# Exchanging two projections between attention stages: group B's queries go to stage B, group C's gate goes to stage A

## The chip, the core and the metric

The kernel runs on one core of one Trainium2 chip. The metric is the device time of one execution in microseconds: the median of three runs of the kernel before is 923.14 us (922.13 to 925.34). Engines have short names: PE is TensorE's matmuls and PEld its weight loads, DVE is VectorE, ACT is ScalarE, POOL is GpSimd, SP is SyncE, which here issues the DMAs.

## What is computed

Two layers of one block, on 512 latent tokens and 256 context tokens of width 1024, one batch, float32:

```
h  = rms_norm(x, norm_g[l]) * (1 + sc) + sh          # hc likewise from ctx
qa, ka, va, ga, qb, kb, vb, gb, qn, kn, vn, gn = split(h @ w_in[l])
ya = rms_norm(diff_attend(rope(norm(qa)), ka_all, va_all, lam)) * (1 - lam_init) * silu(ga)
yb = gqa_attend(rope(norm(qb)), kb_all, vb_all) * silu(gb)
yn = neighbourhood_attend(norm(qn), norm(kn), vn, kn_c, vn_c, rpb) * silu(gn)
x  = x + gt * (concatenate([ya, yb, yn]) @ w_out[l])
```

Group A is differential attention with 4 heads of 64 (two score maps each), group B is grouped-query attention with 6 query heads on 2 key heads, group C is neighbourhood attention with 6 heads, a window of 8 x 16 and a learned bias. Latent queries also attend to all context keys. In layer 0 the context stream has attention and an update of its own; in layer 1 it has only keys and values left to give.

## The kernel before, in words

**Tiles.** Tokens are cut into six tiles of 128, numbered j: 0 to 3 are latent, 4 and 5 are context. The columns of the input projection are cut into chunks (`CH`): `b0` is keys and values of group B, `b1` its queries, `gb` its gate, `c0`, `c1`, `c2` are keys, values and queries of group C, `gn` its gate. `b1`, `gn`, `gb`, `c0`, `c1` and `c2` are 384 columns wide. In layer 1 `b1`, `c2` and the gates have latent tiles only (`ctx_cols`, line 647).

**One projection tile** (`proj`, line 709): 24 matmuls, three for each of eight slices of the inner dimension (lines 679 to 681), because inputs and weights are split into a high and a low part. It is yielded in four quanta. Then `evac` (line 657) takes the result from its PSUM bank, of which the pool psP has two, which it shares with a few small uses. Weights come as pieces (`WStream`, line 60): SP loads raw, ACT makes the high part (line 89), POOL or DVE the low part (line 92). Six pieces are held; a piece is split when an old one is done with. In stage A all low parts fall to POOL, in stage B every second one goes to DVE (`VSHARE`).

**Evacuation of queries or keys** (`qk_evac`, line 451): ACT copies the tile into one of five buffers named xn (462) and squares it (464), DVE sums the squares (465). For group A and B's latent tiles POOL does the turn of the rotary embedding: two products into tb, one of two buffers (485, 487), a product (489, every fourth one on DVE) and a sum (490); other keys, and B's context queries, get one product on POOL (492). After every second tile, or the last, POOL raises the pair's means to the power -1/2 (163); then for each tile DVE scales (498), ACT casts to float16 (515, 523), DVE takes the rest (516, 524), and SP issues a transposing DMA into stB or a big tile (530, 531, 534), from which the scores read.

**Evacuation of a gate** (`gate_evac`, line 597): tanh on ACT (600), one operation on DVE into tb (602), and a DMA into the DRAM tensor g_d (606). `gate_load` (964) brings it back when a unit group needs it; if it isn't there yet, `attn` pumps the projections on.

**Attention units** (`attn`, line 975): scores on PE into one of two psS tiles (775), maximum on DVE (830; 827 with the bias for group C), exponent on ACT (844), high part on ACT (864), low part on POOL (865), a transposing DMA into pt (867), values on PE (900, 901), evacuation (906). The low part is one step behind the scores and the values four steps. Group A also combines its two maps on DVE (860).

**Stages and order.** `both` (line 1054) runs the units of one group and, in between, a list of chunks (`fill`, line 1031), so that after each unit a due share of the quanta has been emitted. Stage A runs group A's units with the list `FA`, stage B group B's with `FB`, stage C group C's with `FC` (turning of outputs and the output projection). `both` has a parameter `lead`, which is 0 everywhere: so many quanta are emitted ahead of the first unit. The order of the weight pieces follows the same lists (`ORDER`). When the list of stage B is through, the high and low inputs are free and the outputs' tiles take their place (line 1073). Group C's bias table is loaded into the buffer that held group B's queries and keys (lines 984 to 987). The emitted program is then ordered for each engine at compile time by a list scheduler with a timeline of its own (line 1353); scores have a priority 400 places ahead of their place (line 779). Each engine then runs its own list in that order.

```
FA = ["b0", "b1", "gb"]
FB = ["c0", "c1", "c2", "gn"]
...
js = (4, 5, 0, 1, 2, 3) if c == "gn" else range(6)
...
both(l, "A", FA)
both(l, "B", FB)
```

Of the kernel before, what the change touches and what calls it, by code (L numbers as in the profile page):

```python
# [116 lines left out]
def tile_hybrid_block(ctx: ExitStack, tc: tile.TileContext, xT_d, cT_d, ng_d, w_ada, bT_d, w_in, w_out,  # L117
# [11 lines left out]
    def sb(shape, dt=F32, tag="", bufs=1):  # L129
        return pool.tile(shape, dt, tag=tag, bufs=bufs, name=tag)  # L130
# [38 lines left out]
    def big(s, dt=F32, shape=None):  # L169
        return sb(shape or [128, KT, SW[s]], dt, "bigL" if s == 0 else "bigC", 3)  # L170
# [89 lines left out]
        next(st["ada"], None)  # L260


    FA = ["b0", "b1", "gb"]
    FB = ["c0", "c1", "c2", "gn"]
    FC = ["y", "o"]
    YE = 2
    F1 = ["a1", "ga"]
    ORDER = [c for c in ["a0"] + F1 + FA + FB + FC if c in CH]
    VCOL = {"a0": (256, 384), "a1": (0, 128), "b0": (128, 256), "c1": (0, 384)}
# [13 lines left out]
    for l in range(DEPTH):  # L283
        for c in ORDER:
            n, c0 = CH[c][1], sum(v[1] for k, v in CH.items() if k < c)
# [96 lines left out]
    def open_norm():  # L382
        nbuf["t"] = sb([128, 2 * NT], F32, "stB")
# [225 lines left out]
    def open_y(l):  # L609
        for k in "hl":  # L610
            yT[k] = [big(0, F32R)] + ([big(1, F32R)] if l == 0 else [])
# [35 lines left out]
    def ctx_cols(l, c):  # L647
        n = CH[c][1]
        if l == 0:
            return n  # L650
        return {"a0": 384, "a1": 128, "b0": 256, "b1": 0, "c0": 384, "c1": 384, "c2": 0}.get(c, 0)

    def tiles_of(l, c):
        js = (4, 5, 0, 1, 2, 3) if c == "gn" else range(6)
        return [(j, CH[c][1] if j < 4 else ctx_cols(l, c)) for j in js if j < 4 or ctx_cols(l, c)]

    def evac(l, c, j, n, ps, last, tag=None):
# [74 lines left out]
    def units(l, g):  # L732
        us, cs = [], []
        for j in range(4):
            for u in range(4 if g == "A" else NH[g]):
                us.append(dict(g=g, j=j, lat=True, segs=[2 * u, 2 * u + 1] if g == "A" else [u]))
        if l == 0:
            for j in (4, 5):
                if g == "A":
                    cs += [dict(g=g, j=j, lat=False, segs=[2 * h, 2 * h + 1]) for h in range(4)]  # L740
                else:
                    cs += [dict(g=g, j=j, lat=False, segs=[3 * i, 3 * i + 2, 3 * i + 1]) for i in range(2)]
        return cs + us if g == "C" else us + cs
# [279 lines left out]
    def run(gen):  # L1023
        for _ in gen:
            pass

    def n_quanta(l, chunks):
        return sum(4 * len(tiles_of(l, c)) if c in CH else (6 if l == 0 else 4) * 2 if c == "y" else
                   8 if c == "n" else 8 * (4 if l == 0 else 2) for c in chunks)

    def fill(l, toks):
        for c in toks:
            if c in CH:
                yield from proj(l, [c])
            elif c == "y":
                n = 6 if l == 0 else 4
                for j in range(0, n, 2):
                    y_pair(l, j)
                    yield
                    yield  # L1040
                for j in range(n):
                    if (l, "B", j) not in turned:
                        y_build(l, "gb", j)
                    yield
            elif c == "n":
                for db in range(KT):
                    while any((l, "C", j) not in turned for j in range(3)):
                        yield
                    out_head(l, db)
                    yield  # L1050
            else:
                yield from out_parts(l)

    def both(l, g, chunks, lead=0):
        share.phase = g
        f = fill(l, chunks)
        nf = n_quanta(l, chunks)
        na = len(units(l, g)) + 4
        for _ in range(lead):
            next(f, None)  # L1060
        done = [lead]

        def pump():
            next(f)
            done[0] += 1

        st["pump"] = pump
        for x, _ in enumerate(attn(l, g)):
            want = min(nf, lead + (nf - lead - REST.get(g, 0)) * (x + 1) // (na - (YE if g == "B" else 0)))
            while done[0] < want:  # L1070
                next(f, None)
                done[0] += 1
            if g == "B" and done[0] >= nf and st.get("y") != l:
                run(f)
                open_y(l)
                st["y"] = l
        run(f)
# [115 lines left out]
    if True:  # L1193
        cT = sb([128, KT, 2], F32, "cT")
        SP.dma_start(out=cT, in_=cT_d)
        x = [big(0), big(1)]
        for h in range(4):
            for st_, t0, w in streams:
                SP.dma_start(out=x[st_][:, 2 * h:2 * h + 2, :], in_=xT_d[:, 2 * h:2 * h + 2, t0:t0 + w])

        warm = psS.tile([128, 1024], F32, tag="s", name="warm")
        for h, n in ((1, 2), (2, 1), (3, 1)):
            for _ in range(n):
                PE.matmul(warm[:, 0:512], lhsT=ident, rhs=x[0][:, 2 * h, :], start=True, stop=True)
        SP.dma_start(out=ng, in_=ng_d)
        SP.dma_start(out=bT, in_=bT_d)
        V.tensor_tensor(out=sel, in0=ident[:, 0:2], in1=ident[:, 32:34], op=ALU.add)
        V.tensor_tensor(out=sel, in0=sel, in1=ident[:, 64:66], op=ALU.add)
        V.tensor_tensor(out=sel, in0=sel, in1=ident[:, 96:98], op=ALU.add)
        th = sb([128, KT, 2], F32, "th")  # L1210
        A.activation(out=th, in_=cT, func=AF.Tanh, scale=0.5)
        V.tensor_scalar(out=th, in0=th, scalar1=1.0, scalar2=0.5, op0=ALU.add, op1=ALU.mult)
        V.tensor_tensor(out=cS[:, :, 0:2], in0=th, in1=cT, op=ALU.mult)
        V.tensor_scalar(out=bT1, in0=bT[:, :, 8:16], scalar1=1.0, scalar2=None, op0=ALU.add)
        open_norm()
        for kt in range(KT):
            for st_ in range(2):
                norm_acc(x[st_][:, kt, :], kt, st_, True)
        ada0 = [ada_load(0, (8, 0))]
        W.advance(1)  # L1220
        for kt in range(1, KT):
            ada0.append(ada_load(0, (8 + kt, kt), kt % 3 == 2))
            if kt % 2 == 1 and kt < 7:
                W.advance(kt // 2 + 2)
        ada_pair(ada0[0])
        rs = norm_both()
        for st_ in range(2):
            hT[st_] = (big(st_, F32R), big(st_, F32R))

        def before0(gi, kt):  # L1230
            if kt:
                ada_pair(ada0[kt])
            for st_ in range(2):
                build_h(0, st_, kt, x[st_], rs[st_])
            if kt == 5:
                layer_consts(0)

        st["ada"] = ada_blocks([(0, b) for b in range(16, 24)] + [(1, b) for kt in range(KT) for b in (8 + kt, kt)]
                               + [(1, b) for b in range(16, 24)])
        share.phase = "1"  # L1240
        proj_first(0, "a0", [[0, 1, 2, 3, 4, 5]], before0)
        for _ in range(AK[0][0] + 1):
            ada_step()
        for l in range(DEPTH):
            share.phase = "1"
            st["cad"] = AK[l][1]
            run(fill(l, F1))
            st["cad"] = AK[l][2]
            both(l, "A", FA)
            st["cad"] = AK[l][3]  # L1250
            both(l, "B", FB)
            while st["done"] < (24 if l == 0 else 32):
                ada_step()
            st["cad"] = 0
            both(l, "C", FC + ["n"] * (l + 1 == DEPTH))
            if l + 1 == DEPTH:
                out_tail(l)
                break
            x = [big(0), big(1)]
            open_norm()  # L1260
            rs = [None, None]
            for db in range(KT):
                out_final(l, db, 1, x[1])
            rs[1] = norm_finish(1)
            for db in range(KT):
                out_final(l, db, 0, x[0])
            hT[1] = (big(1, F32R), big(1, F32R))
            for kt in range(KT):
                prio(-800)(build_h)(l + 1, 1, kt, x[1], rs[1])

            def before1(gi, kt):
                if gi == 1:
                    if kt == 0:
                        rs[0] = norm_finish(0)
                        hT[0] = (big(0, F32R), big(0, F32R))
                    prio(-800)(build_h)(1, 0, kt, x[0], rs[0])

            proj_first(1, "a0", [[4, 5], [0, 1, 2, 3]], before1)
# [81 lines left out]
```

## Time and profile before

| what | us |
|---|---|
| median of three runs | 923.14 |
| the profiled execution's own time | 924.36 |
| its span, first to last instruction | 922.5 |
| mean granted TensorE clock | 0.952 of full speed |
| layer 0: first scores of group A, of B, latent ones of C | 108.5, 260.3, 408.0 |
| layer 1: the same | 599.5, 722.8, 807.9 |

A row of the profile gives line, engine, operation and tiles (written <- read, by the program's names), shapes, how often, then busy time and mean, then the idle time of the engine just before with what ended it. A row in order of time gives start and duration in microseconds first. In a row of a stretch of time each engine's busy microseconds stand with its number of instructions in brackets, then the granted clock, the DMA engines' mean busy share, and GB/s. A letter q behind an engine's name is its sequencer.

### The profile page before, as it was taken

What the parts mean: (1) busy time and instruction counts of PE and PEld (TensorE: products, weight loads), DVE (VectorE), ACT (ScalarE), POOL (GpSimd) and SP (SyncE); (2) the same over time, 40 slices, a digit from 0 to 9 for tenths busy, and PEclk for the clock granted to TensorE, in tenths of its full rate; (3) what the DMA queues carried; (4) which work ended last, traced back from release to release, by engine and by line L of the source; (5) the groups of instructions that cost most, each with busy time, mean ns of one, the idle gap of its engine ahead of it and who ended that gap; (6) DMA issues with size and microseconds to landing.
All of it is one profiled execution on the core that took longest, in us unless ns stands there. A gap on an engine that the chain in (4) does not pass through costs nothing. (4 is left out here: it accounts for less than half of the span.)

```text
span 922.5 us, 17964 instructions
## 1 busy us (share of the span) xinstructions
PE 825.3 (89%) x6386; PEld 706.9 (77%) x6386; DVE 679.0 (74%) x1306; ACT 592.4 (64%) x1269; POOL 541.3 (59%) x502
## 2 busy tenths in 40 slices
PE   5898997996998899897999989989959999988988
PEld 3787876895987789785778889879849878865767
DVE  5985787988678866558656797789877967656843
ACT  5334577784887687477653445478758988839830
POOL 2638855899698565435330047938988886634420
PEclk9899999998999999898999989989969999997989
DMA  9834895645979996998898713784557899996642
GB/s 328 306 97 126 202 214 141 139 95 134 193 162 222 202 223 173 219 259 215 184 211 237 258 52 101 185 185 102 133 128 175 149 190 246 231 260 171 152 91 83
DMA packets 307049, 165.46 MB, mean 179 GB/s; under 512 B 256528, under 2 KB 275216, under 8 KB 306704
## 3 DMA queue, kind: packets, MB, share of 16 engines
q1 hardware_dynamic: 306960, 164.33, 73.7%
q8 instruction: 50, 0.82, 0.4%
q14 instruction: 39, 0.32, 0.1%
HBM read 86.55 MB, written 15.47 MB: 111 GB/s over the span
## 5 line engine op out<-in xcount | busy, mean ns | idle before, releaser
L865 POOL TENSOR_TENSOR hl<-p,hl 128x768 f16<-128x768 f32 (+3 forms) x138 | 203.6, 1480 | 164.9 <-ACT hl L864 148.8
L679 PE MATMUL proj<-whi,bigL 128*128 128x384 f32 (+1 forms) x592 | 203.0, 344 | 8.4 <-DVE tb L602 4.2
L680 PE MATMUL proj<-wlo,bigL 128*128 128x384 f32 (+1 forms) x592 | 199.4, 337 | 0.8 <-POOL wlo L92 0.7
L681 PE MATMUL proj<-whi,bigL 128*128 128x384 f32 (+1 forms) x592 | 197.3, 335 | 0.0
L844 ACT ACTIVATE p<-sc,nb,gsc 128x768 f32<-128x768 f32 (+3 forms) x200 | 166.4, 846 | 10.6 <-DVE p L860 4.7
L830 DVE TENSOR_REDUCE mx<-sc 128x1 f32<-128x768 f32 (+2 forms) x128 | 118.7, 932 | 33.2 <-PE sc L775 33.0
L679 PEld LDWEIGHTS proj<-whi,bigL 128*128 128x128 f32 x592 | 115.2, 195 | 18.7 <-DVE tb L602 5.9
L864 ACT CAST hl<-p 128x768 f16<-128x768 f32 (+3 forms) x144 | 104.1, 726 | 38.5 <-DMA pt<-hl 22.5
L680 PEld LDWEIGHTS proj<-wlo,bigL 128*128 128x128 f32 x592 | 115.5, 195 | 3.9 <-POOL wlo L92 1.5
L681 PEld LDWEIGHTS proj<-whi,bigL 128*128 128x128 f32 x592 | 114.6, 194 | 2.8 <-issue 2.0
L92 POOL TENSOR_TENSOR wlo<-raw,whi 128x768 fp32r<-128x768 f32 (+1 forms) x44 | 83.4, 1902 | 40.3 <-ACT whi L89 37.5
L89 ACT CAST whi<-raw 128x768 fp32r<-128x768 f32 (+1 forms) x104 | 80.3, 780 | 28.4 <-DMA raw<-in_w_in_dram 14.0
L900 PEld LDWEIGHTS <-pt 128*128 128x128 f16 x736 | 65.5, 99 | 35.3 <-DMA pt<-hl 20.9
L679 PE MATMUL proj<-whi,bigC 128*128 128x384 f32 (+2 forms) x224 | 76.0, 339 | 1.0 <-ACT xn L462 1.0
L92 DVE TENSOR_TENSOR wlo<-raw,whi 128x768 fp32r<-128x768 f32 (+1 forms) x60 | 64.9, 1085 | 15.9 <-ACT whi L89 14.4
L680 PE MATMUL proj<-wlo,bigC 128*128 128x384 f32 (+2 forms) x224 | 74.8, 334 | 0.0
L163 POOL TENSOR_TENSOR rsqb<-rsqb,half 128x12 f32<-128x12 f32 (+2 forms) x25 | 68.4, 2737 | 10.0 <-DVE rsqb L162 9.2
L681 PE MATMUL proj<-whi,bigC 128*128 128x384 f32 (+2 forms) x224 | 74.1, 333 | 0.0
L901 PEld LDWEIGHTS <-pt 128*128 128x128 f16 x736 | 66.0, 100 | 4.3 <-issue 2.2
L832 ACT ACTIVATE nb<-mx,lnp,gsc 128x1 f32<-128x1 f32 (+1 forms) x104 | 39.7, 386 | 36.5 <-DVE mx L830 24.4
L775 PE MATMUL sc<-bigL 128*128 128x512 f16 (+4 forms) x184 | 46.4, 312 | 18.0 <-ACT p L844 17.2
L900 PE MATMUL pv<-vA,pt 128*128 128x128 f16 (+2 forms) x424 | 51.3, 228 | 9.6 <-DMA pt<-hl 9.2
(320 smaller groups left out, 2031.5 us busy)
## 6 DMA issues: line engine op xcount, KB each, us to landing
raw<-in_w_in_dram SPq DMA_DIRECT2D x64, 384.0 KB, 4.0
adw<-in_w_ada_dram SPq DMA_DIRECT2D x68, 256.0 KB, 3.6
raw<-in_w_out_dram SPq DMA_DIRECT2D x16, 384.0 KB, 4.7
raw<-in_w_in_dram SPq DMA_DIRECT2D x16, 256.0 KB, 3.1
g_d<-tb SPq DMA_DIRECT2D x20, 192.0 KB, 2.7
gt<-g_d SPq DMA_DIRECT2D x18, 192.0 KB, 3.4
hl<-in_w_ada_dram SPq DMA_DIRECT2D x12, 256.0 KB, 5.2
pt<-in_w_ada_dram SPq DMA_DIRECT2D x12, 256.0 KB, 5.2
```

The source lines that it names most:

```text
L89: self.nc.scalar.copy(out=hi, in_=raw2)
L92: self.share("W").tensor_tensor(out=lo, in0=raw2, in1=hi.bitcast(F32), op=ALU.subtract)
L163: G.tensor_tensor(out=y, in0=x, in1=half[:, 0:n], op=ALU.pow)
L679: PE.matmul(ps, lhsT=xh, rhs=hi, start=(kt == 0), stop=False)
L680: PE.matmul(ps, lhsT=xh, rhs=lo, start=False, stop=False)
L681: PE.matmul(ps, lhsT=xl, rhs=hi, start=False, stop=(kt == KT - 1))
L830: V.tensor_reduce(out=mx[:, 0:ns], in_=ps[:, 0:w * ns].rearrange("p (a b) -> p a b", b=w), axis=AX.X, op=ALU.max)
L844: A.activation(out=p[:, w * x:w * x + w], in_=u["ps", i][:, w * x:w * x + w], func=AF.Exp, bias=u["nb", i][:, x:x + 1], scale=lc[l]["sc"][ ...
L864: A.copy(out=hl[:, 0:n], in_=p)
L865: lo_eng.tensor_tensor(out=hl[:, n:2 * n], in0=p, in1=hl[:, 0:n], op=ALU.subtract)
L900: PE.matmul(po[r, :], lhsT=pt[:, b, r], rhs=V_[:, vt, c0:129], start=first, stop=False)
L901: PE.matmul(po[r, 0:65 - c0], lhsT=pt[:, nb + b, r], rhs=V_[:, vt, c0:65], start=False, stop=stop)
```

## The change

`b1` leaves `FA` and becomes the first chunk of `FB`; `gn` leaves the end of `FB` and takes the place of `b1` in `FA`. Stage B is given a lead of nine quanta, which is two tiles of `b1` and the first quarter of the third. `c2`, now the last chunk of `FB`, gets the tile order that `gn` had, context tiles first; `gn` keeps it. Nothing else is touched: the same tiles are projected and evacuated by the same instructions.

```diff
-    FA = ["b0", "b1", "gb"]
-    FB = ["c0", "c1", "c2", "gn"]
+    FA = ["b0", "gn", "gb"]
+    FB = ["b1", "c0", "c1", "c2"]
...
-        js = (4, 5, 0, 1, 2, 3) if c == "gn" else range(6)
+        js = (4, 5, 0, 1, 2, 3) if c in ("c2", "gn") else range(6)
...
             both(l, "A", FA)
             st["cad"] = AK[l][3]
-            both(l, "B", FB)
+            both(l, "B", FB, 9)
```

## The prediction

> **What bounds the kernel now.** I read the page first, for the busy shares, then cut the trace into the attention stages, then into ten-microsecond pieces, and last read single engines in order of time where the pieces stood out.
>
> ```profile
> PE 825.3 (89%) x6386; PEld 706.9 (77%) x6386; DVE 679.0 (74%) x1306; ACT 592.4 (64%) x1269; POOL 541.3 (59%) x502
> ```
>
> TensorE leads, so time is lost only where it stops or slows. The stages follow from where the scores run; the scores of stage B are the ones that read stB:
>
> ```profile
> L775 PE MATMUL sc<-stB x216: 269/273/390, 260.3 to 804.4; 128*128 128x512 f16 x96, 128*128 128x256 f16 x12
> ```
>
> The next rows give length, then busy time with instructions of PE, PEld, DVE, ACT, POOL, then the granted clock. They are, in layer 0, stage A, two pieces of it and stage B; then the same four of layer 1.
>
> ```profile
> 108.00:260.00 152.00, 133.07 (x1032) 116.87 (x1032) 128.29 (x213) 115.37 (x297) 116.31 (x117) 0.97 0.71 161
> 208.00:218.00 10.00, 5.71 (x38) 4.65 (x39) 10.00 (x9) 3.21 (x8) 10.00 (x6) 1.00 0.44 94
> 218.00:228.00 10.00, 7.31 (x29) 6.34 (x28) 7.14 (x10) 6.61 (x16) 9.16 (x7) 0.66 0.72 214
> 260.00:408.00 148.00, 137.11 (x1151) 119.01 (x1150) 101.97 (x192) 106.47 (x187) 89.41 (x64) 0.98 0.91 207
> 600.00:723.00 123.00, 106.46 (x748) 94.97 (x747) 102.88 (x157) 94.89 (x220) 96.74 (x96) 0.90 0.60 140
> 670.00:680.00 10.00, 2.16 (x15) 1.11 (x14) 6.75 (x7) 7.34 (x18) 10.00 (x7) 0.65 0.43 100
> 680.00:690.00 10.00, 7.18 (x27) 6.49 (x25) 8.76 (x11) 3.55 (x10) 8.05 (x8) 0.50 0.45 121
> 723.00:808.00 85.00, 81.75 (x666) 70.60 (x665) 62.45 (x94) 72.94 (x122) 63.76 (x43) 1.00 1.02 214
> ```
>
> Each stage A has one twenty-microsecond hole in TensorE while POOL is full. Elsewhere stage A of layer 0 does (1032-67) matmuls in 132 us, 7.31 a microsecond; the 67 in the hole are worth 9.2 us, so the hole costs 10.8. In layer 1 it is (748-42)/103 = 6.85 a microsecond, 42 are worth 6.1, and the hole costs 13.9. Together 24.7 us. Stage B has no such hole: TensorE is busy 137 of 148 and 82 of 85 us.
>
> What fills POOL in the first hole, and what VectorE does then:
>
> ```profile
> 208.80 1.99 POOL L92 TENSOR_TENSOR wlo<-raw,whi 128x768 fp32r<-128x768 f32 x1
> 210.75 1.33 POOL L489 TENSOR_TENSOR xn<-xn,t1Bq 128x384 f32<-128x384 f32 x1
> 212.04 3.95 POOL L92 TENSOR_TENSOR wlo<-raw,whi 128x768 fp32r<-128x768 f32 x2
> ```
> ```profile
> 212.09 2.19 DVE L516 TENSOR_TENSOR stg<-xn,stg 128x384 f16<-128x384 f32 x1
> 214.20 2.59 DVE L860 SCALAR_TENSOR_TENSOR p<-p,dn,p 128x768 f32<-128x768 f32 x1
> ```
> ```profile
> 219.26 0.59 PE L775 MATMUL sc<-bigL 128*128 128x512 f16 x1 [3.33 <-ACT p L844]
> ```
> ```profile
> 683.87 0.69 PE L679 MATMUL proj<-whi,bigL 128*128 128x384 f32 x1 [2.81 <-DVE tb L602]
> ```
>
> POOL is turning group B's queries (t1Bq) between weight splits (L92). VectorE's two-input operations stretch beside it, maxima and exponents come late, and TensorE waits for a score bank (3.33 us) or, in layer 1, for a gate tile's tb, a buffer that the turn of the queries uses too (2.81 us). How far the stretch belongs to a busy POOL is shown by the subtraction of line 516 in stage A of layer 0, where it follows group B's queries, and then in stage B:
>
> ```profile
> L516 DVE TENSOR_TENSOR stg<-xn,stg 128x384 f16<-128x384 f32 x6 | 7.6, 1267 | 1.3 <-ACT stg L515 1.2
> ```
> ```profile
> L516 DVE TENSOR_TENSOR stg<-xn,stg 128x384 f16<-128x384 f32 x6 | 3.1, 550 | 1.5 <-ACT stg L515 1.5
> ```
>
> 1267 ns against 550 for the same work.
>
> **The change, part by part.** TensorE's projections cancel: gn and b1 are both 384 columns wide, six tiles each in layer 0 and four in layer 1. So do the weights: as many pieces are loaded and split in each stage, in the same place of the stream. What changes places is the evacuation. For group B's queries POOL has
>
> ```profile
> L485 POOL TENSOR_TENSOR tb<-xn,t2Bq x8: 582/623/922, 184.6 to 676.8; 128x192 f32<-128x192 f32 x8
> L487 POOL TENSOR_TENSOR tb<-xn,t2Bq x8: 590/602/1296, 185.2 to 677.3; 128x192 f32<-128x192 f32 x8
> ```
> ```profile
> L489 POOL TENSOR_TENSOR xn<-xn,t1Bq x6: 996/1004/1330, 192.8 to 683.4; 128x384 f32<-128x384 f32 x6
> ```
> ```profile
> L163 POOL TENSOR_TENSOR rsqb<-rsqb,half 128x12 f32<-128x12 f32 x4 | 9.4, 2359 | 0.4 <-DVE dn L858 0.4
> L492 POOL TENSOR_TENSOR xn<-xn,gs 128x384 f32<-128x384 f32 x4 | 4.2, 1046 | 0.1
> L490 POOL TENSOR_TENSOR xn<-xn,tb 128x384 f32<-128x384 f32 x4 | 4.0, 1008 | 0.0
> ```
>
> The four latent tiles of a layer cost 4 x (0.62 + 0.60 + 1.01) + 3 x 1.00 (one product in four of line 489 is VectorE's) = 11.9 us. Layer 0 adds two context tiles, 2 x 1.05, and three powers, 3 x 2.36: 21.1 us in all. Layer 1 has two powers: 16.6 us. A gate tile has nothing on POOL, one tanh on ScalarE and on VectorE
>
> ```profile
> L602 DVE SCALAR_TENSOR_TENSOR tb<-sq,proj 128x384 f32<-128x384 f32 x4 | 2.2, 555 | 7.7 <-ACT sq L600 7.7
> ```
>
> 0.56 us, less than line 516 alone took in stage A. On SP's queue gn's writes of g_d come into stage A, b1's DMA transposes leave it.
>
> *Stage A, gain.* Without 21 of 116 and 17 of 97 us POOL is no longer full, and the turn no longer shares tb with gb's tiles. Bounds: nothing (splits and line 860 alone still fill those spots) and all 24.7 us, or slightly more if VectorE's relief shows elsewhere. I take four fifths, -20 us, since the query work is what stands between the splits in the holes; splits and line 860 stay for the last fifth. Next in line is TensorE itself, dense in the rest of the stage.
>
> *Stage B, loss by POOL.* It rises to 110.5 of 148 us in layer 0 and 80.4 of 85 in layer 1, where part of it falls ahead of the stage, behind the lead. Queued behind it on POOL are the subtractions of the probabilities, and behind those SP's transposes and the value products. Bounds: nothing, and the whole 24.7 us. Line 516 in stage B lies at the unhindered end, so I stay near that: +3 and +4.
>
> *The handover from A to B.* The first scores now wait for two b1 tiles: copy, square, turn, power, two VectorE passes, a cast, a transpose. From the second tile's copy to its cast the trace has two cases, b1 on a full POOL and c2 on a quiet one:
>
> ```profile
> 649.37 0.48 ACT L462 COPY xn<-proj 128x384 f32<-128x384 f32 x1
> ...
> 671.81 0.51 ACT L515 CAST stg<-xn 128x384 f16<-128x384 f32 x1
> ```
> ```profile
> 376.46 0.47 ACT L462 COPY xn<-proj 128x384 f32<-128x384 f32 x1
> ...
> 384.50 0.91 ACT L515 CAST stg<-xn 128x384 f16<-128x384 f32 x2
> ```
> ```profile
> DMA to landing us min/median/max: 2.4/3.4/5.8
> ```
>
> 22.4 and 8.0 us; a subtraction and a landing add about 4, so 26 or 12. I take 17, for a POOL between the two. The cover is projection. TensorE starts one such matmul every 0.17 us,
>
> ```profile
> 664.06 0.34 PE L680 MATMUL proj<-wlo,bigL 128*128 128x384 f32 x1
> 664.23 0.34 PE L681 MATMUL proj<-whi,bigL 128*128 128x384 f32 x1
> ```
>
> 24 to a tile, 4.1 us. Nothing but the five xn buffers and two banks holds back four more tiles, 16 us. So I cost the handover at nothing; without cover it is 8 to 22 us a layer (12 or 26 less one tile).
>
> *The end of stage B.* c2 now stands last, and stage C's latent scores need its chain. In layer 0 the quiet chain, 12 us, has the last two tiles as cover, 8 us: +4 (bounds 0 and 12). In layer 1 stage C waits for the bias table anyway, whose load sits on SP's queue behind a gate write:
>
> ```profile
> 821.95 0.52 SPq L606 DMA_DIRECT2D g_d<-tb  x1
> 822.52 0.45 SPq L985 DMA_DIRECT2D stB<-in_btab_dram  x1
> ```
>
> Stage B's last scores began at 804.4, so it went out 18 us later than it could. I cost this end at nothing; c2's transposes may hold it as long (bound +4), or it goes out half of that earlier (bound -9).
>
> Sum: -20 + 7 + 4 = -9. The profiled execution took 924.4 us (span 922.5), so 915.4; the median of the runs shown lies 1.2 below it: **914 us**.
>
> **The rivals.** *The load only moves.* Stage B pays back the 20 us. For it: its POOL share in layer 1 would be 95%. Against it: stage B has no line 860, and half of its splits are on VectorE. With 0 to 4 us for the end, 923 to 927: 925. The Trainium skill (SBUF — State Buffer, section "SBUF: two separate sides") speaks for this one: VectorE operations with two SBUF inputs and GpSimd operations take an exclusive lock on a shared port, and the loser blocks, so a moved operation would block as long elsewhere. The two rows of line 516 agree with a lock, but also show that it bites only where POOL is busy.
>
> *Slower: the first scores of stage B arrive late.* If TensorE's order holds one tile instead of four between the pair and those scores, it stops in both layers; it decides from a chain longer than the work placed ahead. With the middle of 8 and 22 less what the tail of stage A covers, 12 a layer: -20 + 24 + 4 = +8, 931 us. For it: the order is fixed at compile time, and real chains ran to 26 us. Against it: layer 0 has slack, with only projections left at the end of its stage B. Row 219.26 and the 0.50 clock of 680 to 690 show that a stop is followed by slow matmuls. That is the clock gate of the Trainium skill (TensorE: Matmul & The Clock Gate, section "What's actually happening"), which halves the clock after an idle stretch; by it each stop would carry some 3 us more (an estimate from that 0.50), 937 us instead of 931.
>
> *More than forecast: the table goes out early.* -9 - 9 = -18, 905 us.
>
> **How the numbers follow.** Forecast 0.55, load only moves 0.17, late scores 0.20, early table 0.08. The forecast's own range is 904 to 922. Over all I give 902 to 931: it leaves out a stage A that gains everything with the early table, and late scores at the long chain. About 0.3%, 2.8 us, is what a measurement of this kernel can tell from no change. Faster: 0.95 of the forecast, 0.2 of the second, all of the fourth: 0.64. Within: 0.03 + 0.08 + 0.01 = 0.12. Slower: 0.24.
>
> **What would show it.** Right: no ten-microsecond piece of either stage A below 6 us of PE with POOL full; stage A about 10 us shorter in each layer; the t1Bq products after the last scores of stage A have begun; stage B within 4 us of its length. Wrong: holes in stage A as before (the splits were the cause), TensorE idle ahead of the first stB scores with a transpose as releaser (late scores), new holes in stage B beside line 489 (load moved).

## The result, and the profile after

The changed kernel takes 928.96 us (median of eight runs, 924.27 to 933.80) against 922.83 for the kernel before beside it: 1.0063 times as long, 95% interval 1.0042 to 1.0084. Measured again it was 1.0077 (1.0052 to 1.0102). The forecast was 914 us and faster; the change is slower by 6 to 7 us. The profiled execution of the first measurement took 933.8 us (span 932.0), the longest of its eight; that of the second took 925.1 (span 923.3), the shortest of its ten. What both show is taken as the change's; where they differ, both are given. Ratios, here and below, leave out the executions that ran in a visibly slower state, one each of three of the variants.

The totals hardly move. The row of busy times in the profile after:

```profile
PE 832.1 (89%) x6386; PEld 711.4 (76%) x6386; DVE 679.1 (73%) x1306; ACT 589.1 (63%) x1269; POOL 544.2 (58%) x502
```

The same stretches as in the prediction, of the profile after: stage A of layer 0 with the two pieces that held its hole; the piece from the last scores of A to the first of B; from there to the first latent exponent of stage C, and two pieces of that; from there to layer 1's first scores; then stage A of layer 1, the piece where its hole would now be, and its stage B to the same point.

```profile
108.00:264.00 156.00, 143.05 (x1127) 127.48 (x1120) 116.60 (x210) 113.29 (x290) 105.31 (x117) 0.97 0.70 167
208.00:218.00 10.00, 9.18 (x64) 8.36 (x62) 7.09 (x11) 7.50 (x17) 9.67 (x10) 1.00 1.04 227
218.00:228.00 10.00, 10.00 (x73) 9.06 (x72) 6.89 (x14) 7.99 (x26) 3.94 (x4) 1.00 0.49 121
245.00:264.00 19.00, 18.11 (x143) 16.44 (x141) 11.79 (x24) 7.51 (x21) 18.50 (x26) 1.00 0.54 143
264.00:430.00 166.00, 141.96 (x1158) 120.50 (x1157) 116.31 (x215) 113.11 (x207) 102.05 (x69) 0.92 0.88 190
284.00:294.00 10.00, 6.21 (x42) 4.72 (x42) 6.56 (x8) 6.04 (x12) 9.84 (x9) 0.67 0.92 143
334.00:344.00 10.00, 7.03 (x36) 6.42 (x37) 7.55 (x24) 6.75 (x11) 4.91 (x3) 0.66 1.04 220
430.00:613.00 183.00, 172.19 (x1239) 147.72 (x1238) 132.24 (x291) 94.67 (x212) 80.04 (x83) 0.93 0.70 179
613.00:726.00 113.00, 105.64 (x785) 94.72 (x784) 96.07 (x147) 91.33 (x213) 86.83 (x85) 0.98 0.68 158
683.00:693.00 10.00, 10.00 (x77) 8.99 (x76) 7.84 (x13) 9.35 (x21) 7.20 (x9) 1.00 0.58 160
...
726.00:844.00 118.00, 100.46 (x769) 85.30 (x767) 90.50 (x126) 87.13 (x146) 85.00 (x59) 0.91 0.89 205
```

For three of these the prediction has no row of the kernel before that ends at the same event:

```profile
260.00:411.00 151.00, 140.11 (x1176) 120.97 (x1174) 104.03 (x198) 108.07 (x190) 91.06 (x65) 0.98 0.92 210
411.00:599.00 188.00, 174.38 (x1307) 150.48 (x1305) 138.61 (x307) 99.32 (x221) 81.03 (x85) 0.96 0.71 180
723.00:835.00 112.00, 100.63 (x812) 86.33 (x810) 77.81 (x120) 85.20 (x144) 71.82 (x47) 0.96 1.01 228
```

The holes of stage A are gone: 9.18 and 10.00 us of TensorE stand where 5.71 and 7.31 stood, 10.00 where it was 2.16. From event to event the program now goes so:

| from | to | before | after, first and second execution |
|---|---|---|---|
| A's first scores | B's first scores, layer 0 | 151.8 | 155.2, 153.8 |
| B's first scores | C's first latent exponent, layer 0 | 151.3 | 166.8, 162.8 |
| that | A's first scores, layer 1 | 187.9 | 182.1, 179.0 |
| A's first scores | B's first scores, layer 1 | 123.3 | 112.8, 112.5 |
| B's first scores | C's first latent exponent, layer 1 | 112.7 | 118.5, 118.5 |

Layer 1 gains 4.7 to 5.0 us. Layer 0 loses 4.6 to 13.1, and it is there that the two executions differ. In layer 0 three things show.

*The handover.* Stage A itself, from its first to its last scores, is 11.0 and 12.8 us shorter. But from its last scores to the first of B it is now 19.3 us (19.8) instead of 4.9. TensorE isn't idle there (18.11 of 19): it does projections, small matmuls into `ada` and the last values of group A, but no scores. The matmul counts of the rows tell where they come from: 95 more ahead of B's first scores than before (1127 against 1032), 18 fewer from there to C's first exponent (1158, 1176) and 68 fewer in the stretch behind it (1239, 1307). About half of the 95 are projection. Counted by their starts, 681 projection matmuls now come ahead of B's first scores instead of 634, and 457 instead of 490 from there to C's first exponent. The 47 more are about two tiles, as many as the pair of `b1` that these scores need.

*Two stops in stage B.* TensorE waited there for transposed probabilities, by the table of waits from B's first to its last scores, of the profile before and then of the profile after (total, times, longest):

```profile
PE pv L900 <- DMA pt<-hl: 0.8, 1, 0.8
```
```profile
PE pv L900 <- DMA pt<-hl: 11.0, 4, 6.5
```

In the second execution it was 9.0 us in three. What stood ahead of the two long ones on POOL, then the two stops of TensorE with SP's queue ahead of the second, in order of time:

```profile
282.77 2.26 POOL L163 TENSOR_TENSOR rsqb<-rsqb,half 128x12 f32<-128x12 f32 x1
285.15 3.88 POOL L865 TENSOR_TENSOR hl<-p,hl 128x768 f16<-128x768 f32 x2
...
327.52 2.27 POOL L163 TENSOR_TENSOR rsqb<-rsqb,half 128x12 f32<-128x12 f32 x1
329.75 3.54 POOL L865 TENSOR_TENSOR hl<-p,hl 128x768 f16<-128x768 f32 x2
```
```profile
288.11 0.29 PE L900 MATMUL pv<-vB,pt 128*128 128x129 f16 x1 [3.79 <-DMA pt<-hl]
```
```profile
327.53 4.68 SPq L867 DMA_TRANSPOSE pt<-hl  x1
...
332.92 5.39 SPq L867 DMA_TRANSPOSE pt<-hl  x2
```
```profile
336.97 0.29 PE L900 MATMUL pv<-vB,pt 128*128 128x129 f16 x1 [6.51 <-DMA pt<-hl]
```

Each time a power of 2.3 us is queued right ahead of the subtraction of the probabilities; their transposes go out late, and TensorE waits for their landing. The first power is that of group B's last pair of queries. The second is one of the keys `c0`, and the queries put it there: `c0` now follows them. Its powers in the kernel before, and the first of them after:

```profile
258.58 2.44 POOL L163 TENSOR_TENSOR rsqb<-rsqb,half 128x12 f32<-128x12 f32 x1 [0.44 <-DVE dn L858]
272.62 2.27 POOL L163 TENSOR_TENSOR rsqb<-rsqb,half 128x12 f32<-128x12 f32 x1
292.74 2.45 POOL L163 TENSOR_TENSOR rsqb<-rsqb,half 128x12 f32<-128x12 f32 x1
```
```profile
295.04 2.27 POOL L163 TENSOR_TENSOR rsqb<-rsqb,half 128x12 f32<-128x12 f32 x1 [0.48 <-DVE rsqb L162]
```

At 258.58 stage B hadn't begun to need POOL; all three of `c0`'s powers now come 35 to 39 us later (295.0, 311.6, 327.5), among the subtractions. But a power in such a place isn't enough for a stop. In the kernel before a subtraction follows the power of 292.74 at once, at 295.15, and TensorE's waits for transposes stay at 0.8 us. SP's queue has a part in the second stop: the three transposes in the rows took 4.68 and 5.39 us of it, where the median of all 144 is 1.40.

*The clock.* The ten-microsecond pieces with the two stops have a granted clock of 0.67 and 0.66, where all of 260 to 360 had 1.00 before. From 288 to 295 it is 0.55, from 337 to 344, behind the second stop, 0.64. So a stop costs itself and the slower matmuls behind it. Altogether TensorE's idle time between B's first scores and C grew from 10.9 (151 - 140.11) to 24.0 us, and the mean clock fell from 0.98 to 0.92. Most of the growth is waiting for transposed probabilities, 13.3 us in that stretch against 2.6 before.

In layer 1 the bias table did go out early, at 818.65, a microsecond behind B's last scores instead of 18. What is late next is `c2`, as the prediction's bound for that end had it, the first scores of C:

```profile
839.18 0.59 PE L775 MATMUL sc<-bigL 128*128 128x256 f16 x2 [4.64 <-DMA bigL<-stg]
```

The second execution has 4.8 there. From B's last scores to C's first exponent it is 26.6 us instead of 31.1.

### The profile page after: what moved, and what is told of

Read it like the earlier page. It is cut to its first block, busy times and chain, and to the rows that moved or that the text cites. A ratio compares the mean times of both kernels' runs of the same rounds, so it can differ in the third digit from the quotient of the medians.

```text
span 932.0 us, 17981 instructions
## 1 busy us (share of the span) xinstructions
PE 832.1 (89%) x6386; PEld 711.4 (76%) x6386; DVE 679.1 (73%) x1306; ACT 589.1 (63%) x1269; POOL 544.2 (58%) x502
## 5 line engine op out<-in xcount | busy, mean ns | idle before, releaser
L900 PEld LDWEIGHTS <-pt 128*128 128x128 f16 x736 | 67.9, 102 | 52.7 <-DMA pt<-hl 40.2
L89 ACT CAST whi<-raw 128x768 fp32r<-128x768 f32 (+1 forms) x104 | 80.4, 780 | 30.4 <-DMA raw<-in_w_in_dram 14.4
L92 DVE TENSOR_TENSOR wlo<-raw,whi 128x768 fp32r<-128x768 f32 (+1 forms) x60 | 70.8, 1181 | 12.0 <-ACT whi L89 9.1
L163 POOL TENSOR_TENSOR rsqb<-rsqb,half 128x12 f32<-128x12 f32 (+2 forms) x25 | 67.5, 2699 | 20.2 <-DVE rsqb L162 19.8
L901 PEld LDWEIGHTS <-pt 128*128 128x128 f16 x736 | 68.1, 102 | 3.6 <-issue 1.3
L775 PE MATMUL sc<-bigL 128*128 128x512 f16 (+4 forms) x184 | 48.6, 331 | 17.8 <-ACT p L844 12.8
L900 PE MATMUL pv<-vA,pt 128*128 128x128 f16 (+2 forms) x424 | 53.4, 230 | 8.5 <-DMA pt<-hl 7.5
```

What stands on the lines that cost most here:

```text
L89: self.nc.scalar.copy(out=hi, in_=raw2)
L92: self.share("W").tensor_tensor(out=lo, in0=raw2, in1=hi.bitcast(F32), op=ALU.subtract)
L163: G.tensor_tensor(out=y, in0=x, in1=half[:, 0:n], op=ALU.pow)
L900: PE.matmul(po[r, :], lhsT=pt[:, b, r], rhs=V_[:, vt, c0:129], start=first, stop=False)
L901: PE.matmul(po[r, 0:65 - c0], lhsT=pt[:, nb + b, r], rhs=V_[:, vt, c0:65], start=False, stop=stop)
```

## The experiments

All ratios are to the kernel before, timed beside it; in microseconds they are the ratio's excess times 923. Of each variant only one execution is profiled, and executions scatter by some 5 us: times are taken from the ratios, places from the profiles. In the expectations LOAD means that POOL's work for the queries costs in stage B what it cost in stage A, END that `c2`'s chain stands last, BORROW that the projections which cover the handover are missing later, and POWER that powers stand ahead of the probabilities on POOL.

**The changed kernel once more** (no edit).

> The changed kernel once more, unchanged, because its profiled execution (span 932.0) was the longest of its eight runs (924.3 to 933.8). All theories: median 925 to 930 us. What is structural must come again: stage A 10 to 11 us shorter a layer, the first scores of layer 0's stage B 15 to 20 us after the last of stage A, stage B 8 us or more longer a layer. If stage B is less than 5 us longer a layer in this execution, its loss in the first profile was scatter of that execution.

1.0077 (1.0052 to 1.0102). Handover (19.8) and both longer stages B (+8.1, +10.2 from first to last scores) came again: structural, as expected.

**The two ends alone, and together.** `c2` last, in the kernel before:

```diff
-    FB = ["c0", "c1", "c2", "gn"]
+    FB = ["c0", "c1", "gn", "c2"]
...
-        js = (4, 5, 0, 1, 2, 3) if c == "gn" else range(6)
+        js = (4, 5, 0, 1, 2, 3) if c in ("c2", "gn") else range(6)
```

> Only the end of stage B of the change: the kernel before, with gn ahead of c2 instead of behind it (and c2's context tiles first). Groups, stage A and POOL's work per stage stay. Theory END (c2's chain stands last and stage C waits for it): +4 to +8 us, 927 to 931. Theory LOAD (the queries' work on POOL and the rest of their evacuation cost in stage B what they cost in stage A): within 2 us of before. Theory BORROW (projections used up between stages A and B are missing at the end of stage B): within 2 us of before as well, as nothing is pulled forward.

1.0101 (1.0069 to 1.0133), +9.3 us: END, and more than twice the prediction's +4. In the one profiled execution (929.1 us) B's first scores to C's first exponent are 2.4 and 3.4 us longer; the rest of the 9.3 us has no place in it that stands out.

The lead alone, in the kernel before:

```diff
-            both(l, "B", FB)
+            both(l, "B", FB, 9)
```

> Only the lead of the change: the kernel before with nine of stage B's projection steps (two tiles of c0 and a quarter) placed ahead of its first scores. Theory BORROW: the 9 us of projection are missing at the end of stage B, so layer 0 loses 4 to 8 us there and layer 1 up to 4: 927 to 933. Theories LOAD and END: within 2 us of before.

1.0061 (1.0040 to 1.0083), +5.6 us. The price is BORROW's, but its place isn't: layer 0 kept its length from B's first scores to C (152.3 against 151.3), and layer 1 lost 5.0 (117.7 against 112.7), all of it ahead of B's last scores. Its mechanism isn't seen either. TensorE's order has 634 of layer 0's projection matmuls ahead of B's first scores with the lead as without it, so nothing was pulled ahead of them. In layer 1 TensorE idles no longer than before (11.3 us against 11.4 in that stretch), but 310 projection matmuls instead of 279 stand between B's first and last scores. Why this costs 5.6 us at the end of the program is open.

Both edits, without the exchange of b1 and gn:

> The kernel before with both of the change's edits at the ends of stage B and without its swap of b1 and gn: c2 last, and nine projections ahead. Alone they cost 1.010 and 1.006. Theory END AND LEAD (projections that cover c2's chain are used up ahead): they add up or more, 936 to 943. Rival (they share one cost): 928 to 934.

1.0153 (1.0114 to 1.0191), +14.1 us: they add up (5.6 + 9.3 = 14.9). What the changed kernel has beyond these two, the exchange itself, is thus worth 1.0153 to 1.0077, about -7 us, if the lead costs the same with `b1` at the head of the list.

**What stage A's holes are worth.** The kernel before, with group B's queries neither turned nor raised to their power:

```diff
-        qk_turn(l, g, w, j, xt, nh, d)
+        if (g, w) != ("B", "q"):
+            qk_turn(l, g, w, j, xt, nh, d)
...
-        G.tensor_tensor(out=y, in0=x, in1=half[:, 0:n], op=ALU.pow)
+        G.tensor_tensor(out=y, in0=x, in1=half[:, 0:n], op=op)
...
-        r = rsqrt(ss[:, :m], m, 1.0, d * EPS * QS * QS)
+        r = rsqrt(ss[:, :m], m, 1.0, d * EPS * QS * QS, op=ALU.mult if (g, w) == ("B", "q") else ALU.pow)
```

> The kernel before with the turn of group B's queries and their power left out (the power a product), in stage A where it does them. Theory POOL MADE THE HOLES: both holes of stage A go, stage A is 9 to 12 us shorter a layer, and as nothing else is touched the gain reaches the end: 899 to 908 us. Rival (splits and the other evacuation fill the same spot, and the change gained in stage A by something else, such as the gate tiles' place): stage A is less than 5 us shorter a layer, 914 to 922. Rival (a shorter stage A is given back later, by the weights' stream or the bias table): stage A shorter by 9 or more, time above 912.

0.9911 (0.9878 to 0.9945), -8.2 us, with the holes gone. The windows that held them, in this profile:

```profile
208.00:218.00 10.00, 10.00 (x68) 9.41 (x67) 9.18 (x14) 8.49 (x20) 9.75 (x11) 1.00 0.69 188
218.00:228.00 10.00, 9.63 (x65) 8.32 (x63) 8.52 (x17) 7.90 (x21) 3.07 (x4) 1.00 0.92 162
...
670.00:680.00 10.00, 9.94 (x66) 8.74 (x65) 9.85 (x15) 7.80 (x19) 3.74 (x3) 1.00 0.84 161
680.00:690.00 10.00, 9.73 (x74) 8.84 (x73) 5.04 (x9) 9.81 (x24) 9.84 (x10) 1.00 0.77 220
```

So the queries' work on POOL was needed for them. But stage A is 7.6 and 7.7 us shorter, 15.3 in all, and 8.2 reach the end: of what was expected this is nearest to the third. In the profiled execution the give-back lies in layer 0, where B's first scores to C took 163.0 us instead of 151.3, although nothing of its content changed; layer 1 keeps all it gains. That execution took 918.9 us, the longest of its runs, so the size of this give-back is uncertain. No power of the queries stands in this kernel, and its stage B of layer 0 still has a wait of 4.7 us for transposes (the line numbers of this profile are one higher):

```profile
PE pv L901 <- DMA pt<-hl: 5.1, 2, 4.7
```

A third of stage A's weight splits off POOL, in the kernel before:

```diff
-          "W1": (1, 1)}
+          "W1": (1, 1), "WA": (1, 3)}
```

> The kernel before, with one weight split in three of stage A moved from POOL to VectorE and nothing else changed: it relieves POOL in stage A by about as much as the change does without touching stage B. If the full POOL was what made the holes in stage A, stage A shrinks 6 to 11 us a layer less what VectorE loses, and stage B keeps its length: 905 to 918 us. If it was the queries' own chain (or VectorE is as full as POOL there), no change or slower: 921 to 930.

1.0072 (1.0047 to 1.0097): the second case. Stage A is 4.4 and 2.7 us shorter, and layer 1's stage B, which the edit doesn't touch, 11.5 longer.

The queries as the last step of stage A, in the kernel before:

```diff
-    FA = ["b0", "b1", "gb"]
+    FA = ["b0", "gb", "b1"]
```

> The kernel before with gb projected ahead of b1 in stage A, nothing else changed: the queries are still turned in stage A, but as its last step, 20 us later. If the hole of stage A is the queries' work on a POOL that is full of splits all through the stage, the hole moves with the queries and the stage is as long: 921 to 926. If it is their coincidence with work at that spot (key norms of b0, gate tiles that share the buffer tb), the hole shrinks and stage A with it, 912 to 919. If the chain of the last pair is not covered by the tail of stage A, the first scores of stage B come late by 5 to 15 us a layer: 930 to 945.

1.0217 (1.0183 to 1.0251), +20 us: by its time the third case. From A's last scores to B's first it is 13.2 and 8.0 us instead of 4.9 and 3.2, so 8.3 and 4.8 more, where the prediction bounded an uncovered handover at 8 to 22 a layer. But in layer 0 stage A is 9.7 us shorter, which is the second case, so B's first scores come no later (150.2 us after A's, 151.8 before); in layer 1 they come 4.0 later. Most of the 20 us is thus not explained by the handover. The shorter stage A also bears on the holes: in the ten microseconds from 208, and again from 218, TensorE is busy 9.63 and 10.00 us here, beside a POOL busy 9.75 and 10.00. So in layer 0 a full POOL alone doesn't make the hole; it took the queries' work at that spot.

**POOL's part in stage B.** The changed kernel without the turn of group B's queries:

```diff
-        qk_turn(l, g, w, j, xt, nh, d)
+        if (g, w) != ("B", "q"):
+            qk_turn(l, g, w, j, xt, nh, d)
```

> The changed kernel without the rotary turn of group B's queries and the product of its context tiles (four POOL operations a latent tile, one a context tile, left out): some 12 to 14 us of POOL a layer are gone from the start of stage B and nothing is put in their place. Theory LOAD: stage B, 112 and 92 us from first to last score, shrinks by 6 us or more in each layer, and the time falls by 10 to 20 us, to 909 to 919. Theory END: stage B shrinks by 0 to 3 us, and the time stays above 924.

1.0012 (0.9992 to 1.0032), 6.0 us below the changed kernel. That is less than LOAD's 10 to 20, and stage B is still 6.4 and 11.8 us longer than in the kernel before, in layer 1 no shorter than in the changed kernel; the time is END's. The powers still stand ahead of subtractions of the probabilities in this kernel, at 292.48 and 311.25 us for example, but no long wait is left in layer 0's stage B (line numbers one higher again):

```profile
PE pv L901 <- DMA pt<-hl: 6.0, 4, 2.0
```

Then without their power (the power a product, as above):

> The changed kernel with the power on GpSimd that ends a pair of group B's query tiles (2.3 us each, three in layer 0 and two in layer 1) replaced by a product of the same operands; so the queries' scale is left out. In the changed kernel's stage B such a power stands on POOL right ahead of a subtraction of the probabilities, and TensorE then waits for pt<-hl transposes (11.0 us in layer 0, 4.5 in layer 1; 0.8 and 2.6 in the kernel before). Theory POWER BLOCKS PROBABILITIES: without it these waits fall by half or more in layer 0, and the time falls 4 to 7 us, to 923 to 926. Theory SP QUEUE (the transposes themselves are late behind weight loads on SP's queue): the waits stay, and the time is within 2 us of the changed kernel, 928 to 931.

1.0007 (0.9986 to 1.0029), 6.5 us below the changed kernel's 1.0077, in the span that POWER named. TensorE's waits in layer 0's stage B:

```profile
PE pv L900 <- DMA pt<-hl: 3.2, 5, 1.0
```

3.2 us instead of 11.0 and 9.0, no long one left, and from B's first scores to C it is 151.9 us again. In layer 1 nothing of this shows: up to C's first exponent the waits are 11.8 us (10.0 in the changed kernel) and the stretch is 120.5 us long (118.5). Both left out:

> The changed kernel with the turn of group B's queries and their power both left out (the power a product again): the queries cost POOL almost nothing, in either stage. Without the turn alone the changed kernel took 1.0012 of the kernel before. Theory POOL (all that the change pays back in stage B is POOL's share of the queries): the sum of both leave-outs, 917 to 921, stage B at 100 and 82 us. Theory END AND LEAD (c2 last cost 1.010 and nine projections ahead cost 1.006 when done alone): stage B recovers only in part, 921 to 926, with layer 1's stage B still over 88 us.

1.0003 (0.9973 to 1.0033): END AND LEAD by the time, with stage B at 111.5 and 87.8 us (the forecast had layer 1 just over 88). Either relief takes all of POOL's part, 6 to 7 us; they don't add. Without POOL's part the change gains nothing, so the rest of stage A's gain is spent elsewhere. The same work left out of the kernel before gave 0.9911, so with it out of both kernels the change costs 8.5 us.

**Where c2 stands, and what hides it.** The changed kernel with `c2` ahead of `c1`:

```diff
-    FB = ["b1", "c0", "c1", "c2"]
+    FB = ["b1", "c0", "c2", "c1"]
...
-        js = (4, 5, 0, 1, 2, 3) if c in ("c2", "gn") else range(6)
+        js = (4, 5, 0, 1, 2, 3) if c in ("c1", "gn") else range(6)
```

> The changed kernel with the last two chunks of stage B in the other order: group C's queries (c2) third, its values (c1) last, context tiles first. Theory END (c2's long evacuation chain now stands between the last projection and stage C's latent scores): the first latent exponent of stage C in layer 0, 430.7 us in the changed kernel, comes 10 to 15 us earlier, and the time falls by 6 to 10 us, to about 921. Theory LOAD (the cost sits in stage B, where group B's queries meet the other work on POOL): stage B keeps its length (last scores 375.6 and 817.4 us), the time falls by 0 to 3 us, about 927.

1.0086 (1.0062 to 1.0110): no gain, although in layer 0 the first exponents of C come earlier (406.7 us against 430.7 and 425.3). In this execution layer 1 loses it: from B's first scores to C's first exponent it takes 128.8 us instead of 118.5. The same, with turn and power left out:

> The changed kernel with c2 ahead of c1 and with the turn and the power of group B's queries left out (the power a product). With c2 ahead of c1 alone it took 1.0086 of the kernel before, with the leave-out alone 1.0003. If both c2's place and POOL cost what they cost alone in the kernel before, this is 8 to 12 us below the kernel before: 911 to 916. If the end of stage B only changes its releaser (values late in place of queries): 921 to 927.

0.9883 (0.9853 to 0.9913), -10.8 us. So `c2`'s place is worth 11 us when POOL's part is out (1.0003 to 0.9883) and nothing when it is in, and POOL's part is worth 18.7 us with `c2` ahead (1.0086 to 0.9883) and 6.8 with it last. Each hides the other. Against the kernel before with the same work left out (0.9911) the interval leaves no difference. Exchanging gn with gb instead of with b1, that is gn in stage A and gb first in stage B, with `c2` last and no lead:

```diff
-    FA = ["b0", "gn", "gb"]
-    FB = ["b1", "c0", "c1", "c2"]
+    FA = ["b0", "b1", "gn"]
+    FB = ["gb", "c0", "c1", "c2"]
...
-            both(l, "B", FB, 9)
+            both(l, "B", FB)
```

> Half of the change: group B's queries stay in stage A, group C's gate goes to stage A as in the change, and group B's gate (gb) goes to stage B in place of the queries, with no lead; c2 is last in stage B as in the change. POOL has in both stages what it had in the kernel before. Theory LOAD: stage A keeps a hole as before (about 25 us over both layers), stage B is as long as before (about 100 and 82 us from first to last score), the time is that of the kernel before give or take 4 us plus what the end costs. Theory END: layer 0's stage C still starts late, its latent exponents 10 us or more behind the kernel before at an equal end of stage B, so 925 to 932.

1.0169 (1.0135 to 1.0202), +15.6 us and above both forecasts: the queries stay in stage A, which keeps its length in layer 0 (145.3 us against 146.8). The loss shows in layer 0 behind it, where B's first scores to C's first exponent take 166.7 us instead of 151.3.

**VectorE as a way out.** The changed kernel with the turn's products of line 489 and sums of line 490 in stage B moved to VectorE:

```diff
-          "W1": (1, 1)}
+          "W1": (1, 1), "TB": (1, 1), "RB": (1, 1)}
```

> The changed kernel with the product and the sum of group B's turn (lines 489 and 490) on VectorE in stage B, so that POOL has 1.2 us a tile left of it in place of 3.2. Theory LOAD: half of what leaving the turn out gains, 5 to 10 us, to about 921, unless VectorE is the engine that limits; then no gain. Theory END: no change, 929.

1.0220 (1.0189 to 1.0252), 13 us above the changed kernel and above every case that was expected. With a third of the probabilities' subtractions in stage B moved there instead:

```diff
-          "W1": (1, 1)}
+          "W1": (1, 1), "HB": (1, 3)}
```

> The changed kernel with every third subtraction of the probabilities (line 865) in stage B moved from POOL to VectorE. Theory POWER BLOCKS PROBABILITIES, or POOL load in general: the waits of TensorE for pt<-hl in stage B fall and the time falls 3 to 6 us, to 924 to 927. Rival (VectorE is busy 74% of stage B and has the maxima to do): the maxima come later, waits for p<-sc take their place, 928 to 934.

1.0130 (1.0100 to 1.0160): the rival's time, but not its way. The waits for transposes fell (3.4 us in layer 0) and the time rose, but TensorE's waits for exponents, which were to take their place, fell as well (1.8 us up to C's first exponent in layer 0, 3.6 in the changed kernel). Last, the power of the queries on VectorE, by a first guess from the number's bits and three Newton steps:

```diff
+    def newton(src, n, mul, add):
...
+        V.tensor_scalar(out=x, in0=src, scalar1=mul, scalar2=add, op0=ALU.mult, op1=ALU.add)
+        V.tensor_scalar(out=y.bitcast(I32), in0=x.bitcast(I32), scalar1=-0.5, scalar2=1597463007.0,
+                        op0=ALU.mult, op1=ALU.add)
+        for _ in range(3):
+            V.tensor_tensor(out=u, in0=y, in1=y, op=ALU.mult)
+            V.scalar_tensor_tensor(out=u, in0=u, scalar=-0.5, in1=x, op0=ALU.mult, op1=ALU.mult)
+            V.scalar_tensor_tensor(out=y, in0=u, scalar=1.5, in1=y, op0=ALU.add, op1=ALU.mult)
...
-        r = rsqrt(ss[:, :m], m, 1.0, d * EPS * QS * QS)
+        r = (newton if (g, w) == ("B", "q") else rsqrt)(ss[:, :m], m, 1.0, d * EPS * QS * QS)
```

with `c2` ahead of `c1`, in the kernel before, and in the changed kernel as it is:

> The changed kernel with c2 ahead of c1 and the power of group B's queries worked out on VectorE in eleven small operations instead of one of 2.3 us on GpSimd; nothing left out. Theory POWER (it is the power ahead of the probabilities that hides what c2's place is worth): most of the 17 us between 1.0086 and 0.9883 come without leaving the turn out, less some 2 us a power on VectorE: 914 to 920 us, faster than the kernel before. Rival TURN (POOL's load as a whole): 924 to 930.

> The kernel before with that power on VectorE and nothing else changed: the turn stays in stage A on GpSimd. With turn and power both left out it took 0.9911. If the power makes the hole: 914 to 919. If the turn does: 921 to 926, as VectorE is 84% busy in stage A and takes some 10 us more.

> The changed kernel with that power on VectorE and c2 last as it is. With the power left out it took 1.0007 of the kernel before. If VectorE has room for it: 922 to 926; if its operations delay the maxima and the copies of stage B: 927 to 932.

1.0169 (1.0139 to 1.0199), 1.0176 (1.0143 to 1.0210), 1.0201 (1.0175 to 1.0226): all above every case that was expected, and 8, 16 and 11 us above the same kernels with the power on POOL. None of the kernels that do all the work beats the kernel before.

## Why the prediction was wrong, step by step

*Stage A, gain: -20.* In its place right. Stage A is 21.8 us shorter in the first execution and 23.9 in the second, the holes are gone, and the queries' work on POOL was needed for them, as named, since leaving it out closes them. (That POOL is full is not enough: with the queries at the end of stage A the spot was full too, and TensorE ran.) As a term of the sum it failed: the same relief without any other edit brought 8.2 us (5 to 11) at the end of the program, not 20. I added a stage's gain as if the stages stood one behind the other with nothing between; in the profiled execution what follows in layer 0 took back what stage A gave. Why it did is open.

*The handover: nothing.* "So I cost the handover at nothing." In layer 1 this held (3.4 us against 3.2). In layer 0 it failed: 14.4 us more. The cover was there, and TensorE was busy under it, but half of what it did there was projection taken out of the stages that follow, and stage B didn't become shorter for it: TensorE idled 24.0 us up to C's first exponent, not 10.9, mostly waiting for transposes. Some came back behind that, where 68 matmuls fewer are left to do and the stretch is 5.8 and 8.9 us shorter, so 6 to 9 us are left if that is set against the handover. That stage B ran short of filling work isn't shown: the lead alone cost 5.6 us without putting a projection ahead of B's first scores.

*Stage B, loss by POOL: +3 and +4.* Leaving out either piece of that part or both gives 6.0 to 6.8 us: the size was right, in part by luck, since it is 18.7 with `c2` ahead of `c1`. In layer 0 the way was the one named, "behind it on POOL are the subtractions of the probabilities, and behind those SP's transposes and the value products". The argument for the size wasn't: line 516 did not stay at the unhindered end. Its rows for group B's queries in the profile after, from 245 to 376 us and from 700 to 818:

```profile
L516 DVE TENSOR_TENSOR stg<-xn,stg 128x384 f16<-128x384 f32 x6 | 4.2, 698 | 0.6 <-ACT stg L515 0.6
```
```profile
L516 DVE TENSOR_TENSOR stg<-xn,stg 128x384 f16<-128x384 f32 x4 | 5.8, 1438 | 0.1
```

In layer 1 1438 ns, more than the 1267 of stage A in layer 0 before: there the stretch moved with the queries. What POOL's part cost in layer 0 came as two stops with a slow clock behind them. A power stood right ahead of each, but the runs don't show it to be the one cause: without the turn, and with the powers in place, the long stops are gone as well.

*The end of stage B: +4.* By the profile it came nearly as written: 55.1 us from B's last scores to C's exponents against 51.3 in layer 0, in layer 1 an early table and then `c2` as releaser, -4.5. By the timing `c2` last costs 9.3 us when it is done alone. Where the other 5 are is open.

*The sum.* Measured one by one, -8.2 (stage A's POOL work), +14.1 (the two ends) and +6.8 (POOL in stage B) make +12.7, against +6.5. The exchange also takes the queries' work on VectorE and ScalarE out of stage A, which the leave-out doesn't, and the terms hide each other, as `c2`'s place and POOL's part do; the missing 6 us weren't split between the two. The steps that failed, and turned the sign, are the two that cost the ends, lead and `c2` last, at 4 together where 14.1 was measured, and the -20 for stage A that was added in full where 8.2 reached the end. How the ends cost that much is open beyond this.

*The rivals.* "The first scores of stage B arrive late" was nearest, 931 us: in layer 0 they do, 14.4 us against its 12, though not with TensorE idle, and in layer 1 they don't. "The load only moves" had the place right (stage B longer by 11.7 and 10.3), but not the cause: with the turn and the power left out stage B is still 11.5 and 6.2 us longer than before. "The table goes out early" came true and brought half of its 9 us.

## What to carry to other kernels

A hole that is closed on the critical engine need not bring its length at the end: here stage A became 15.3 us shorter by leaving work out, and 8.2 us reached the end. So price the stages behind it as well. Work that covers a chain isn't free because the engine is busy: here TensorE was busy through the handover, and the first scores of stage B still came 14 us later behind the last of stage A. When an evacuation is moved, look where its longest operations land in each queue, and what they push back behind them: here either the turn of the queries or their power of 2.3 us, taken out, removed the long stops. Try each edit of a change alone first: both ends of this one cost more than the forecast had for the whole.

## What the runs showed of the hardware

Moving work from POOL, busy for 58 or 59% of these kernels, to VectorE cost time in all six tries. The Newton steps show a part of the reason; their rows in the changed kernel with them, nanoseconds as minimum, median and maximum:

```profile
L174 DVE TENSOR_TENSOR nwt<-rsqb x15: 170/172/1606, 253.0 to 731.4; 128x12 f32<-128x12 f32 x15
```
```profile
L175 DVE SCALAR_TENSOR_TENSOR nwt<-nwt,rsqb x15: 170/172/1792, 253.6 to 732.4; 128x12 f32<-128x12 f32 x15
```
```profile
L176 DVE SCALAR_TENSOR_TENSOR rsqb<-nwt,rsqb x15: 155/172/1605, 253.8 to 732.9; 128x12 f32<-128x12 f32 x15
```

An operation on 12 elements a partition takes 172 ns or, at times, 1.6 us and more, about as long as one of POOL's subtractions of the probabilities (1.77 to 1.94 us each in the rows at 285.15 and 329.75). The Trainium skill (SBUF — State Buffer, section "SBUF: two separate sides") has a lock on a shared port, held for a whole instruction, for VectorE operations with two SBUF inputs against GpSimd's; these rows agree with it. The 45 operations of these rows took 20.6 us together, 4.1 us for each of the five powers that take 2.3 us on POOL; at the median they would have taken 7.7. That these 13 us are the 11 us by which this kernel is slower isn't shown.

The granted clock was 0.66 and 0.67 in the ten microseconds with the end of a stop of 6.5 us and with a stop of 3.8 us. The Trainium skill (TensorE: Matmul & The Clock Gate, section "What's actually happening") has half the clock after a window of some 3.4 us without work; two thirds of such a piece at half clock would give 0.67 (an estimate from that page), so the rows agree with it.
